# A residual kept in DRAM between stages, its SBUF space given to a pool of work tiles

## The chip, the cores and the metric

The kernel runs on one core of a Trainium2 chip. The metric is the device time of one execution in microseconds. TensorE (PE) does the matrix products, VectorE (DVE), ScalarE (ACT) and GpSimd (POOL) the elementwise work; SyncE (SP) issues nearly all transfers, GpSimd those that add while they write.

## What is computed

Two layers over 512 frames of 1024 features, in float32. Each layer has three stages, and behind each stands a layer norm on the residual x:

```python
for i in range(DEPTH):                     # DEPTH = 2, ALPHA = sqrt(2)
    x = layer_norm(ALPHA * x + 0.5 * swiglu(x, gate1[i], up1[i], down1[i]), ...)      # hidden width 2816
    x = layer_norm(ALPHA * x + hybrid_mixer(x, ...), ...)
    ffn = 0.5 * swiglu(x, gate2[i], up2[i], down2[i])
    ple = sigmoid(x @ ple_w_gate[i]) * (p[i] @ ple_w_proj[i])                          # p[i]: 512 x 256
    x = layer_norm(ALPHA * x + ffn + ple, ...)
```

The mixer projects x to 3340 columns and runs three recurrences on them: a retention of 4 heads (with rotary embedding of its queries and keys), a gated linear recurrence of width 384, and a gated delta rule of 6 heads, each in chunks. Their outputs, 1024 wide together, go through w_out.

## The kernel before

**Products.** Every large operand is split into a high part and the rest, so one product of float32 is three matmuls. A weight tile of 128 x 1024 comes from DRAM into one of four raw buffers (`NRAW`), ACT copies the high part into a slot, and VectorE, sometimes GpSimd, or an adding transfer of GpSimd's queue makes the low part in a second slot. The raw buffer is free for the next load when both are done.

**Slots.** Nearly all SBUF space beside constants is a pool of `NSLOT` = 40 slots of 4 KB per partition (128 x 1024 float32). `slots.get` takes the slot that has been free longest, `slots.put` gives one back; two half tiles share a slot (`halves`). Slots hold split weights, the transposed x and its combinations, the hidden units, and all temporaries of the mixer. The residual is apart from this: `xt`, four tiles of 128 frames x 1024, 4 KB each per partition, which live in SBUF for the whole run (L329).

**Planner.** The program is written out by a planner in Python, which keeps an estimated clock for each engine and decides in which order instructions are emitted. The main thread emits the large products (`mm`, L305). Side threads (`spawn`) emit the dependent chains: norms, the delta rule, the gated recurrence, the retention. They give up control at each `yield` and are resumed when their operands should be there. `prefetch` splits further weights while the work on hand is less than a target and slots are free (`can_step`); `room(n)` keeps a side thread from going on before n slots are free; `wait_until` lets the main thread wait, which advances only side threads. The framework below the planner then orders each engine's queue and sets the semaphores: an instruction that is ready can go ahead of earlier ones that are not.

**Stages.** `swiglu` forms the 22 blocks of hidden units with seven products per block, then runs the down projection over 22 blocks: frames 0 to 255 first, frames 256 to 511 seven blocks later (`LAG`). `mixer` projects block by block (`unit`, 24 matmuls of 512 columns each, in the order q, x, l, r, z, g), spawns the chains, and then multiplies with w_out: eight pairs of weight slots for frames 0 to 255, then again for 256 to 383 and 384 to 511. A rotary unit ("r") starts only when five slots are free (L1657). `embed` does the p part and adds it to `xt` (L1758). `norm` does its first instruction on `xt` (L716), then mean, variance, scale and bias in place, then the transposes by TensorE.

**x.** The input x is loaded into `xt` in four transfers of 512 KB, which the code asks for behind the 24th, 27th, 30th and 33rd weight load (L427 to L429).

Of the kernel before, what the change touches and what calls it, by code (L numbers as in the profile page):

```python
# [20 lines left out]
LN_EPS = 1e-5  # L21
LAG = 7
GROUP = 2
NSLOT = 40
NRAW = 4
TARGET = 14.0
LEVELS = (2, 4, 8, 16, 32, 64)
# [82 lines left out]
def tile_trunk(ctx: ExitStack, tc: tile.TileContext, a, out):  # L110
# [215 lines left out]
    id16 = cpool.tile([128, 128], F16, name="id16")  # L326
    cosT = cpool.tile([128, S], F32, name="cosT")
    sinT = cpool.tile([128, S], F32, name="sinT")
    xt = [cpool.tile([128, D], F32, name=f"x{t}") for t in range(4)]  # L329
    cvr = cpool.tile([128, 128], F32R, name="cvr")  # L330
    nea = cpool.tile([128, L, 6], F32, name="nea")
    m8 = cpool.tile([128, 2, L, 3], F32, name="m8")
# [83 lines left out]
    def load_more():  # L416

        while st["loaded"] < len(loads) and (st["loaded"] < NRAW or readers[st["loaded"] - NRAW] == 0):
            src = loads[st["loaded"]]
            r = raw_tile()  # L420
            dst = r.rearrange("p (g c) -> p g c", g=2) if len(src.shape) == 3 else r[:, 0:src.shape[1]]
            nc.sync.dma_start(out=dst, in_=src)
            raws.pop(st["loaded"] - 1 - NRAW, None)
            if st["loaded"] == 12:
                consts()
                spawn(rotary_tables())
            if st["loaded"] in (24, 27, 30, 33):  # L427
                t = (st["loaded"] - 24) // 3
                nc.sync.dma_start(out=xt[t], in_=a["x"][t * 128:(t + 1) * 128, :])  # L429

    def add_one():

# [267 lines left out]
    def free_xT():  # L700
        for kp in range(4):
            slots.put(xh[kp], xl[kp])
            xh[kp] = xl[kp] = None

    def norm(t, acc, c, gb, out=None, halves_done=None, kind="whole"):


        x = xt[t]
        bs = small.tile([128, 2, 6], F32, tag="bs", name="bs")
        mv = small.tile([128, 2], F32, tag="mv", name="mv")  # L710
        rs = small.tile([128, 1], F32, tag="rs", name="rs")
        for h in range(2):
            while halves_done is not None and halves_done[0] <= h:
                yield
            s = slice(h * 512, (h + 1) * 512)
            stt(x[:, s], acc[h], c / ALPHA, x[:, s], MUL, ADD)  # L716
            ps.put(acc[h])
            if halves_done is not None:
                nc.vector.bn_stats(out=bs[:, h, :], in_=x[:, s])
        yield  # L720
        if halves_done is None:
            for h in range(2):
                nc.vector.bn_stats(out=bs[:, h, :], in_=x[:, h * 512:(h + 1) * 512])
        nc.vector.bn_aggr(out=mv, in_=bs)
        spend("D", 1300, [mv], [x])
        rsqrt(rs, mv[:, 1:2], LN_EPS / ALPHA ** 2)
        yield
        if halves_done is not None:
            for h in range(2):
                s = slice(h * 512, (h + 1) * 512)  # L730
                stt(x[:, s], x[:, s], mv[:, 0:1], gb[0][:, s], SUB, MUL)
                stt(x[:, s], x[:, s], rs, gb[1][:, s], MUL, ADD)
                nc.sync.dma_start(out=out[t * 128:(t + 1) * 128, s], in_=x[:, s])
            slots.put(gb[0], gb[1])
            return
        stt(x, x, mv[:, 0:1], gb[0], SUB, MUL)
        yield
        stt(x, x, rs, gb[1], MUL, ADD)
        gb[2] -= 1
        if gb[2] == 0:  # L740
            slots.put(gb[0], gb[1])
        if out is not None:
            nc.sync.dma_start(out=out[t * 128:(t + 1) * 128, :], in_=x)
            return
        yield
        names = [f"A{1 + t // 2}{q}" for q in (1, 2)]
        keep_raw, parts = kind != "whole", True
        while kind == "whole" and xh[0] is None:
            if len(slots.free) >= 8:
                new_xT()  # L750
            else:
                yield
        while kind != "whole" and names[0] not in quad and names[0] not in xr:
            if len(slots.free) >= 4 * parts + 2 * keep_raw:
                for nm in names:
                    if parts:
                        new_quad(nm)
                    if keep_raw:
                        xr[nm] = slots.get([128, 4, 256], F32)
            else:  # L760
                yield
        c = slice(t * 128, (t + 1) * 128) if kind == "whole" else slice(t % 2 * 128, t % 2 * 128 + 128)
        for q in range(2):
            yield from free_bank()
            p = bank()
            pv = p.rearrange("p (k t) -> p k t", k=4)
            for k in range(4):
                f = (4 * q + k) * 128
                ptr(pv[:, k, :], x[:, f:f + 128], ident)
            for i in range(2):  # L770
                src = pv[:, 2 * i:2 * i + 2, :]
                if kind == "whole":
                    hi, lo = xh[2 * q + i][:, :, c], xl[2 * q + i][:, :, c]
                elif parts:
                    hi, lo = (quad[names[q]][i][:, :, j, c] for j in range(2))
                else:
                    continue
                act(hi, src)
                tt(lo, src, f32(hi), SUB)
            if keep_raw:  # L780
                act(xr[names[q]][:, :, c], pv)
            ps.put(p)
            yield


    def swiglu(l, nm, pend, out=None, kind="whole"):
# [116 lines left out]
        for j in range(MT):  # L903
            ws[j] = take()
            if j:
                if j + 1 < MT:
                    split_h(j + 1)
                down(j, (0, 1))
            else:
                split_h(1)  # L910
                down(0, (0, 1))
                last.run("T4")
                free_quads()
            if j >= LAG:
                if j == LAG:
                    get_acc(acc, (2, 3))
                if j == LAG + 3:
                    gb = load_gb(l, nm)
                if j == MT - 1:
                    ths = [spawn(norm(t, acc[t], 0.5, gb, out, kind=kind), urgent=True) for t in (0, 1)]  # L920
                down(j - LAG, (2, 3))
                drop(j - LAG)
# [52 lines left out]
    def mixer(l, pend):  # L975
# [708 lines left out]
        for k in ks:  # L1684
            need(k, first)
            ws[k] = take()
            wo(k, (0, 1))
        spare[0] = 0
        in_mixer[0] = False
        gb = load_gb(l, "ln_mix")  # L1690
        ths = [spawn(norm(t, acc[t], 1.0, gb, kind="both"), urgent=True) for t in (0, 1)]
        for t in (2, 3):
            get_acc(acc, (t,))
            for k in ks:
                need(k, second)
                wo(k, (t,))
                if t == 3:
                    slots.put(*ws[k])
                    slots.put(oT[k])
            ths.append(spawn(norm(t, acc[t], 1.0, gb, kind="both"), urgent=True))  # L1700
# [4 lines left out]
    def embed(l, pend):  # L1705
# [12 lines left out]
        for half in range(2):  # L1718
# [34 lines left out]
            for t in tiles:  # L1753
# [3 lines left out]
                    ps.put(acc[t][h])  # L1757
                tt(xt[t], xt[t], sg[t], ADD)  # L1758
                slots.put(sg[t])
        slots.put(ph, pl)  # L1760
        wait([mix])

# [190 lines left out]
```

## Time and profile before

| | |
|---|---|
| median of 3 runs | 2166.35 us (2161.36 to 2168.34) |
| the profiled execution | 2159.74 us, of which its span is 2158.0 us |
| PE busy | 2115.7 us, 98% |
| DVE, ACT, POOL busy | 1417.5, 1114.7, 343.3 us |
| moved by transfers | 268.38 MB |

The profile is of one execution; its times count from the start of its span. A busy matmul has a modelled end, so matmuls that wait for one another can still read as busy. The stages can be told by the shape of the matmuls: 256 columns in the gate and up products, 512 in the down projections and most of the mixer. In the first layer the mixer runs from about 350 to 673 us, in the second from about 1425 to 1745 us.

### The profile page before, as it was taken

The numbers are of one execution on the slowest core, as the hardware profiler recorded it, in microseconds if no ns is written. First come the engines' busy times: TensorE is split into PE (matmuls) and PEld (weight loads), VectorE is DVE, ScalarE is ACT, GpSimd is POOL, SyncE is SP. The second block draws the span as 40 slices with busy tenths as digits, with TensorE's granted clock in tenths as the row PEclk, the third lists the DMA queues.
The fourth block names the chain that finished last, engine by engine and source line by source line (L and its number), as shares of the span: only waits on it lengthen the run. The fifth ranks groups of instructions, "written<-read, shape, count | busy, mean of one in ns | idle before, by whom it ended". The sixth has DMA issues, their size and how long they took to land.

```text
span 2158.0 us, 35722 instructions
## 1 busy us (share of the span) xinstructions
PE 2115.7 (98%) x14264; PEld 1905.0 (88%) x14264; DVE 1417.5 (66%) x2415; ACT 1114.7 (52%) x1880; POOL 343.3 (16%) x325
## 2 busy tenths in 40 slices
PE   8999999999999999999999999999999999999998
PEld 7999988977778899998899998889777889999986
DVE  7766636878767766673486665378787677666634
ACT  7666532657334666662266664335564247666530
POOL 3111001233221111100011110012333111111000
PEclk9999999999999999999999999999999999999999
DMA  9776532210133576763247765322102336766621
GB/s 283 178 177 171 162 118 79 79 47 11 59 115 113 127 173 165 176 179 115 83 117 172 174 169 164 106 84 69 38 21 66 98 113 146 187 167 165 182 88 40
DMA packets 104343, 268.38 MB, mean 124 GB/s; under 512 B 9328, under 2 KB 11376, under 8 KB 104176
## 3 DMA queue, kind: packets, MB, share of 16 engines
q1 hardware_dynamic: 80416, 201.07, 28.5%
q0 software_dynamic: 23760, 65.02, 16.8%
q8 instruction: 112, 1.84, 0.3%
q14 instruction: 55, 0.45, 0.1%
HBM read 198.95 MB, written 2.10 MB: 93 GB/s over the span
## 4 chain that ended last, share of the span: by engine, by line
PE 86%; DVE 7%; DMA 3%; ACT 2%; POOL 1%; issue 1%; SPq 0%; DVEq 0%; POOLq 0%; ACTq 0%
PE p L305 78%; PE p L259 6%; DVE s L235 4%; PE p L263 2%; DMA raw<-in_wgu_dram 1%; ACT s L217 1%; DMA s<-in_xT_dram 1%; DMA s<-raw 1%; POOL fs L692 1%; DVE s L239 1%; DMA raw<-in_win_fm_dram 0%; ACT L217 0%; DVE x L239 0%; DVE s L1404 0%; POOL s L235 0%
## 5 line engine op out<-in xcount | busy, mean ns | idle before, releaser
L305 PE MATMUL p<-s,s 128*128 128x256 f32 (+1 forms) x12048 | 1945.1, 320 | 14.0 <-ACT s L217 12.6
L305 PEld LDWEIGHTS p<-s,s 128*128 128x128 f32 x12048 | 1710.5, 191 | 170.6 <-ACT s L217 14.2
L217 ACT ACTIVATE s<-raw 128x1024 fp32r<-128x1024 f32 (+2 forms) x521 | 462.1, 911 | 316.9 <-PE p L305 235.4
L235 DVE TENSOR_TENSOR s<-s,s 128x1024 fp32r<-128x1024 f32 (+4 forms) x433 | 383.9, 908 | 182.7 <-ACT s L217 148.0
L217 ACT ACTIVATE s<-s 128x512 fp32r<-128x512 f32 (+5 forms) x485 | 336.6, 709 | 322.0 <-DVE s L235 164.8
L235 DVE TENSOR_TENSOR s<-raw,s 128x1024 fp32r<-128x1024 f32 (+3 forms) x351 | 334.5, 958 | 245.2 <-ACT s L217 191.6
L217 ACT ACTIVATE s<-p 128x256 f32<-128x256 f32 (+5 forms) x740 | 279.0, 407 | 316.2 <-PE p L305 121.7
L436 POOL DMA_DIRECT2D s<-raw x165 | 143.2, 872 | 881.2 <-ACT s L217 694.2
L235 DVE TENSOR_TENSOR s<-p,s 128x256 f32<-128x256 f32 (+4 forms) x376 | 157.1, 432 | 73.9 <-PE p L305 48.3
L259 PE MATMUL p<-s,s 128*128 128x128 f16 (+6 forms) x1496 | 154.2, 250 | 7.8 <-DVE s L235 6.7
L235 DVE TENSOR_TENSOR s<-raw 128x512 f32<-128x512 f32 x168 | 115.0, 686 | 68.7 <-PE p L305 65.0
L692 POOL TENSOR_TENSOR rs<-rs,half_neg 128x1 f32<-128x1 f32 x24 | 34.8, 1450 | 537.5 <-DVE rs L244 537.5
L259 PEld LDWEIGHTS p<-s,s 128*128 128x128 f32 (+1 forms) x680 | 89.9, 195 | 21.6 <-issue 6.3
L239 DVE SCALAR_TENSOR_TENSOR s<-p,vecs,s 128x255 f32<-128x255 f32 (+5 forms) x128 | 69.3, 550 | 19.7 <-PE p L263 14.8
L217 ACT ACT_TABLE_LOAD x48 | 61.6, 1283 | 14.5 <-DVE tails L250 7.2
L235 DVE TENSOR_TENSOR s<-s,p 128x512 fp32r<-128x512 f32 (+3 forms) x92 | 45.7, 502 | 16.6 <-PE p L259 12.9
L259 PEld LDWEIGHTS <-s 128*128 128x128 f16 x816 | 37.4, 101 | 20.7 <-issue 11.5
L235 DVE TENSOR_TENSOR s<-p,lvm 128x512 f16<-128x512 f32 x72 | 48.2, 683 | 10.6 <-PE p L259 10.2
L235 POOL TENSOR_TENSOR s<-s,cst 128x512 f32<-128x512 f32 x26 | 36.8, 1417 | 96.1 <-DVE s L235 70.0
L239 DVE SCALAR_TENSOR_TENSOR x<-p,x 128x512 f32<-128x512 f32 x48 | 31.5, 682 | 29.2 <-PE p L305 29.0
L263 PE MATMUL p<-cst,s 128*128 128x128 f32 x172 | 33.0, 290 | 9.6 <-ACT s L217 5.3
L263 PEld LDWEIGHTS p<-cst,s 128*128 128x128 f32 x172 | 20.5, 145 | 17.5 <-ACT s L217 6.1
(103 smaller groups left out, 663.3 us busy)
## 6 DMA issues: line engine op xcount, KB each, us to landing
raw<-in_wgu_dram SPq DMA_DIRECT2D x172, 512.0 KB, 4.6
raw<-in_ffn_w_down_dram SPq DMA_DIRECT2D x88, 512.0 KB, 3.6
s<-raw POOLq DMA_DIRECT2D x83, 512.0 KB, 5.4
raw<-in_win_fm_dram SPq DMA_DIRECT2D x48, 512.0 KB, 3.6
s<-raw POOLq DMA_DIRECT2D x82, 256.0 KB, 4.2
raw<-in_w_out_dram SPq DMA_DIRECT2D x16, 512.0 KB, 3.6
raw<-in_ple_w_gate_dram SPq DMA_DIRECT2D x16, 512.0 KB, 4.0
s<-in_xT_dram SPq DMA_DIRECT2D x4, 512.0 KB, 6.3
```

What stands on the lines that cost most here:

```text
L217: nc.scalar.activation(out=out, in_=in_, func=func, **kw)
L235: (eng or nc.vector).tensor_tensor(out=out, in0=in0, in1=in1, op=op)
L239: nc.vector.scalar_tensor_tensor(out=out, in0=in0, scalar=scalar, in1=in1, op0=op0, op1=op1)
L259: nc.tensor.matmul(out=out, lhsT=lhsT, rhs=rhs, start=start, stop=stop)
L263: nc.tensor.transpose(out, in_, idn)
L305: nc.tensor.matmul(out=out, lhsT=lhsT, rhs=rhs, start=start, stop=stop, skip_group_check=resumed)
L436: nc.gpsimd.dma_start(out=out, in_=in_, accum_op=ADD)
L692: nc.gpsimd.tensor_tensor(out=dst, in0=dst, in1=e, op=POW)
```

## The change

`xt` is no longer held in SBUF. Four tiles in DRAM (`xd`) keep the residual. `fetch_x(t)` takes a slot and loads tile t into it (the first time from the input), `keep_x(t)` writes the tile to DRAM and gives the slot back. The pool grows from 40 to 44 slots, which is the 16 KB per partition that `xt` had.

- Feed-forward: the four tiles are fetched at iterations `LAG + 4` to `LAG + 7` of the down projection (11 to 14 of 0 to 21).
- Mixer: tiles 0 and 1 are fetched within the products of w_out as soon as five slots beside the spare four are free, at the latest before the norms are spawned; tiles 2 and 3 each just before their own products.
- Norms: after the transposes of a tile the norm keeps it, save after the mixer, where the embedding uses `xt` next and keeps it itself. The last norm writes the output and keeps nothing.

In all 24 fetches, four of which take the place of the loads of the input, and 20 keeps, of 512 KB each.

```diff
-NSLOT = 40
+NSLOT = 44
...
-    xt = [cpool.tile([128, D], F32, name=f"x{t}") for t in range(4)]
+    dpool = ctx.enter_context(tc.tile_pool(name="kept", bufs=1, space=bass.MemoryType.DRAM))
+    xd = [dpool.tile([128, D], F32, name=f"xd{t}") for t in range(4)]
+    xt = [None] * 4
+    x_in = [True] * 4
...
-            if st["loaded"] in (24, 27, 30, 33):
-                t = (st["loaded"] - 24) // 3
-                nc.sync.dma_start(out=xt[t], in_=a["x"][t * 128:(t + 1) * 128, :])
...
+    def fetch_x(t):
+        xt[t] = slots.get([128, D], F32)
+        nc.sync.dma_start(out=xt[t], in_=a["x"][t * 128:(t + 1) * 128, :] if x_in[t] else xd[t])
+        x_in[t] = False
+
+    def keep_x(t):
+        nc.sync.dma_start(out=xd[t], in_=xt[t])
+        slots.put(xt[t])
+        xt[t] = None
...
@@ norm, after the transposes
+            if q == 1 and kind != "both":
+                keep_x(t)
...
@@ swiglu, down projection
+                if LAG + 4 <= j < LAG + 8:
+                    fetch_x(j - LAG - 4)
...
@@ mixer
             ws[k] = take()
+            for t in (0, 1):
+                if xt[t] is None and len(slots.free) >= 5 + spare[0]:
+                    fetch_x(t)
             wo(k, (0, 1))
         spare[0] = 0
         in_mixer[0] = False
+        for t in (0, 1):
+            if xt[t] is None:
+                wait_until(lambda: slots.free)
+                fetch_x(t)
...
         for t in (2, 3):
             get_acc(acc, (t,))
+            wait_until(lambda: slots.free)
+            fetch_x(t)
...
@@ embed
                 tt(xt[t], xt[t], sg[t], ADD)
                 slots.put(sg[t])
+                keep_x(t)
```

## Rows read from the trace of the kernel before

**Rows 1.** The page's head and its part 1: busy time of the engines.

```profile
span 2158.0 us, 35722 instructions
...
PE 2115.7 (98%) x14264; PEld 1905.0 (88%) x14264; DVE 1417.5 (66%) x2415; ACT 1114.7 (52%) x1880; POOL 343.3 (16%) x325
```

**Rows 2.** The page's part 4: the chain that ended last, shares by engine.

```profile
PE 86%; DVE 7%; DMA 3%; ACT 2%; POOL 1%; issue 1%; SPq 0%; DVEq 0%; POOLq 0%; ACTq 0%
```

**Rows 3.** Windows: stretch, its us, busy us (x instructions) per engine, clock, DMA share, GB/s.

```profile
280.00:300.00 20.00, 20.00 (x90) 16.57 (x89) 7.89 (x9) 6.81 (x9) 0.00 (x0) 1.00 0.30 88
```

**Rows 4.** PE timeline, 0 to 62 us; in brackets idle time before, and its releaser.

```profile
37.51 0.73 PE L305 MATMUL p<-s,s 128*128 128x256 f32 x4 [0.33 <-DMA s<-raw]
39.74 12.50 PE L305 MATMUL p<-s,s 128*128 128x256 f32 x102 [1.50 <-ACT s L217]
53.15 0.98 PE L305 MATMUL p<-s,s 128*128 128x256 f32 x6 [0.91 <-ACT s L217]
54.80 7.45 PE L305 MATMUL p<-s,s 128*128 128x256 f32 x60 [0.68 <-DVE s L235]
```

**Rows 5.** The chain in order of time, first 60 us: start, us, what.

```profile
30.78 12.35 DMA s<-raw
...
43.25 8.42 DMA raw<-in_wgu_dram
```

**Rows 6.** DMA issues of the whole run: KB each, median us from issue to landing.

```profile
raw<-in_wgu_dram SPq DMA_DIRECT2D x172, 512.0 KB, 4.6
...
s<-raw POOLq DMA_DIRECT2D x83, 512.0 KB, 5.4
...
x<-in_x_dram SPq DMA_DIRECT2D x4, 512.0 KB, 12.1
...
out_dram<-x SPq DMA_DIRECT2D x3, 512.0 KB, 2.6
```

**Rows 7.** SP's timeline, 28 to 36 us.

```profile
30.83 2.17 SPq L429 DMA_DIRECT2D x<-in_x_dram  x4
```

**Rows 8.** Windows of line L305 alone: stretch, us, PE, PEld, clock, DMA share, GB/s.

```profile
515.00:532.00 17.00, 0.00 (x0) 0.00 (x0) 0.80 0.00 1
1586.50:1603.50 17.00, 0.00 (x0) 0.00 (x0) 0.80 0.01 1
```

**Rows 9.** Windows of all engines, first mixer: PE, PEld, DVE, ACT, POOL, clock, DMA.

```profile
515.00:532.00 17.00, 14.21 (x124) 12.79 (x123) 13.93 (x32) 15.87 (x31) 7.83 (x8) 0.80 0.00 1
532.00:565.00 33.00, 29.57 (x186) 23.82 (x185) 30.62 (x59) 13.16 (x27) 10.49 (x8) 0.97 0.21 65
565.00:600.00 35.00, 34.70 (x200) 29.46 (x198) 22.01 (x46) 14.29 (x23) 9.42 (x9) 0.98 0.21 60
600.00:648.00 48.00, 45.45 (x244) 37.01 (x245) 31.01 (x77) 12.97 (x25) 7.82 (x7) 0.93 0.36 119
```

**Rows 10.** SP's timeline, 470 to 560 us.

```profile
477.71 0.33 SPq L422 DMA_DIRECT2D raw<-in_win_fm_dram  x1
...
534.78 18.01 SPq L422 DMA_DIRECT2D raw<-in_win_fm_dram  x3
```

**Rows 11.** What SP's queue waited for, 470 to 640 us: total, times, longest.

```profile
SPq L422 <- DVE s L235: 126.5, 13, 56.7
```

**Rows 12.** Windows of instructions on x alone: PE, PEld, DVE, clock, DMA.

```profile
380.00:648.00 268.00, 0.14 (x2) 0.00 (x0) 0.00 (x0) 0.97 0.19 61
```

**Rows 13.** The chain in order of time: start of ffn2, start of the second layer.

```profile
739.57 9.42 DMA raw<-in_wgu_dram
...
1110.85 6.86 DMA raw<-in_wgu_dram
```

**Rows 14.** PE timeline, 1095 to 1130 us, with the idle time before.

```profile
1125.58 4.69 PE L305 MATMUL p<-s,s 128*128 128x256 f32 x37 [1.26 <-ACT s L217]
```

**Rows 15.** Groups of VectorE, 520 to 600 us: xcount | busy, mean ns | idle before.

```profile
L235 DVE TENSOR_TENSOR s<-raw,s 128x1024 fp32r<-128x1024 f32 x7 | 8.7, 1244 | 0.5 <-ACT s L217 0.4
...
L235 DVE TENSOR_TENSOR s<-p,cosT 128x512 f32<-128x512 f32 x3 | 2.0, 677 | 0.0
```

## The prediction

> **What bounds the kernel now.** The page comes first [rows 1]: TensorE is busy for 2115.7 us of a span of 2158.0, so idle time alone leaves 42 us to win, both ends of the run included. A busy TensorE is not one at its peak, so the second view is the chain that ended last [rows 2]: 86% of it runs through PE, 7% through VectorE, 3% through DMA. The stages of the feed-forward blocks are closed: a window of 20 us there holds 90 matmuls of 512 columns at full clock, 222 ns each [rows 3], with nothing between them. More slots can give nothing there, since the operands are in time already. What is left lies in three places, which I looked for in the idle gaps of the PE timeline and in the windows: the first 60 us, the two mixers, and the seams between stages.
>
> *The first 60 us.* The PE timeline shows four gaps after 37 us, of 0.33, 1.50, 0.91 and 0.68 us, together 3.42 us [rows 4]. The chain there runs through two transfers, an accumulate of 12.35 us and a weight load of 8.42 us [rows 5]; over the run these take 5.4 and 4.6 us [rows 6]. What is different just then is that the four loads of x go out at 30.83 us, one behind the other [rows 7], and take 12.1 us each to land [rows 6].
>
> *The mixers.* From 515 to 532 us, and again from 1586.5 to 1603.5 in the second layer, the line that does all large products (L305) has not one matmul [rows 8]. In those 17 us TensorE does 124 small matmuls of the side threads, its granted clock averages 0.80, and ACT (15.87 us) and VectorE (13.93 us) carry the chain [rows 9]. Weights are not far away: the queue issues a load of w_in at 477.71 and the next one at 534.78 [rows 10], and of that it waits 56.7 us in one piece for VectorE to split a raw tile [rows 11]. So raw tiles lie there full and are not split. By the code a split asks two slots of the planner, and a rotary unit (L1657) only starts with five free. I read this as a shortage of slots, and it is the place where the change should act; that ACT and VectorE are at 93% and 82% in the same 17 us speaks against it.
>
> **The change part by part.**
>
> *Slots.* x is not touched by any engine's arithmetic from 380 to 648 us [rows 12] (the two matmuls there are the last of a transpose), and the change puts it in DRAM for just such stretches. So the four tiles are really there for the mixer; from the fetch to the next keep the pool has 40 left, as before. Four slots hold two split weights, which are two units of 24 matmuls of 512 columns: 2 x 24 x 0.222 = 10.7 us of TensorE work [rows 3] that can start where L305 has none. A unit also wants slots for its result, so one unit, 5.3 us, is the lower end of what I expect of the mechanism, 10.7 the upper. I take 8 us per layer, 16 in all. If a mixer only swaps one wait for another it is 0, the bound on that side.
>
> *Clock.* [...] I put none of it in the sum, because the clock is also below full at 600 to 648 us (0.93), where L305 is at work. [...]
>
> *The loads of x at the start go.* The first fetch is now asked for in the down projection of the first block, at iteration 11 of 22. 2 MB leave a stretch where transfers set the chain. The two slow transfers were 12.35 - 5.4 = 7.0 and 8.42 - 4.6 = 3.8 us over their usual time [rows 5, 6], more than the 3.42 us of gaps, so these can all close. I take -3 us; bounds 0 and -3.4.
>
> *Fetches.* 24 of 512 KB, four of which replace the old ones. In the feed-forward blocks they are asked for seven iterations ahead of the norm, 7 x 24 x 0.222 = 37 us. In the mixer tiles 0 and 1 are asked for with the products of w_out, at most 96 x 0.222 = 21 us ahead, tiles 2 and 3 at least 48 x 0.222 = 10.7 us ahead. Landing takes 3 to 5 us for such sizes, 12.1 at the most crowded [rows 6]. All hidden; if a slot came free late, the first instruction of the norm would hold up VectorE, with the splits behind it, by some us per stage. None in the sum.
>
> *Keeps.* 20 writes of 512 KB on SP's queue, each behind the last write of x by VectorE; behind it in the queue are weight loads. A late keep holds the loads back by about the norm's own last instructions, some 1 to 3 us, and the loads themselves wait far longer for raw tiles [rows 11]. The framework also orders a queue's transfers by when it thinks they are ready: the x loads went out at 30.8 us, though the code asks for them behind the 24th weight load. The slot is free when the write has landed, 2.6 us by the nearest row, the output's write [rows 6]. What can cost is the seam: the keeps behind the first layer's last norm and behind the embedding fall where the first loads of the next block are on the chain, 6.86 us at 1110.85 and 9.42 at 739.57 [rows 13]. Two keeps there take 2 x 2.6 = 5 us of the same engines, and a seam has little to hide that in: TensorE stands still for 1.26 us just behind the first of the two [rows 14]. Over both seams that is 0 to some 10 us; I take +2, near the lower end, because a load that is late by 2 us mostly meets operands prepared ahead. [...]
>
> *Sum.* -3 - 16 + 2 = -17 us on the profiled execution's 2159.74. That execution is 6.6 us below the median of 2166.35 and just under the lowest run; I put the same difference on the median: **2149 us**. About 6.5 us, 0.3%, is what a measurement of this kernel can tell from no change; the runs shown spread over 7 us.
>
> **The rivals.**
>
> *A, no change.* The gap in the mixer is a dependent chain on ACT and VectorE, and the large products only move within the mixer: whatever TensorE does earlier, it then waits for the side threads at the end. For it: ACT 93% and VectorE 93% busy in 515-532 and 532-565. Against it: VectorE is idle for 13 of 35 and 17 of 48 us after that [rows 9], so the end is not its bound. -3 + 2: 2165 us. The same time follows if the four slots are swallowed by deeper prefetch.
>
> *B, slower.* VectorE is the bound from 532 to 565 (30.62 of 33 us [rows 9]). Two units moved ahead bring it two splits of weights of 1.24 us, and three further passes of about 0.68 each (the cosine product's row) [rows 15]: 2 x 3.3 = 6.6 us in front of the delta threads, in either layer. If the delta threads, not the retention, are what the last products of w_out wait for, this comes out at the end: +13.2 - 3 + 2 = +12, 2178 us. It decides if the 30 us of VectorE idle after 565 lie beyond that chain.
>
> [...]
>
> *D, contention takes it.* The mixers give 16, but both seams lose 7.0 us, as the accumulate beside the loads of x did [rows 5, 6]: -3 - 16 + 14 = -5, 2161 us, within what can't be told.
>
> **How the numbers follow.** Forecast (2140 to 2158) 0.50; A 0.18; D 0.07; B 0.13; C 0.12. The likeliest gives 2149. The range goes from 2131, below most of C, to 2170, above A and D with the spread of the runs; B and a tail of C stay out, under 2 in 10. The forecast's own range is 2140 to 2158. Faster by over 0.3% is the forecast and C with a little of D: 0.63. The same is A, most of D and an edge of the forecast: 0.22. Slower is B and a tail of A: 0.15.
>
> **What would show it.** L305 should have some 24 to 48 matmuls in the 17 us where it has none, and the clock there should be nearer to full. The 57 us between two weight loads in the mixer should shrink. The gaps at 37 to 55 us should be gone, with the accumulate at its usual 5 us. The mixer should be about 8 us shorter from its first product to the embedding's. Reads of x from DRAM should land over 5 us ahead of the norm's first instruction. I am wrong if the mixer is as long as before with L305 moved, if VectorE shows a wait for x, or if the gap of 1.26 us at the second layer's start grows by more than 2 us.

## The result, and the profile after

| | before | after |
|---|---|---|
| median of 3 runs | 2166.35 us | 2187.02 us (2184.68 to 2190.61) |
| the profiled execution, its span | 2159.74, 2158.0 us | 2187.02, 2185.2 us |
| moved by transfers | 268.38 MB | 289.36 MB |

The ratio is 1.0107 (95% interval 1.0076 to 1.0138): slower by 21 us by the medians, 23 by the ratio, where 17 us of gain were forecast. The page of the kernel after, its head, its busy times, its chain by engine and the new transfers, answers to [rows 1, 2, 6]:

```profile
span 2185.2 us, 35799 instructions
...
PE 2125.2 (97%) x14264; PEld 1914.1 (88%) x14264; DVE 1418.6 (65%) x2413; ACT 1125.1 (51%) x1886; POOL 341.4 (16%) x327
...
PE 77%; DVE 9%; DMA 6%; ACT 4%; POOL 2%; issue 2%; SPq 0%; DVEq 0%; ACTq 0%; POOLq 0%
...
xd<-s SPq DMA_DIRECT2D x20, 512.0 KB, 3.1
s<-xd SPq DMA_DIRECT2D x20, 512.0 KB, 3.4
```

The work of each engine is what it was. What grew in the chain is DMA, from 3% to 6%, VectorE, from 7% to 9%, and ScalarE, from 2% to 4%: TensorE is fed later. To see where, take from each trace the start of the same matmul of L305, the k-th of its width (counted from 0, here and below), and subtract the kernel before. The differences of those differences say what each stretch lost (+) or won (-), in us:

```text
                       start  mixer 1  2nd ffn  its rest  layer 2  mixer 2  2nd ffn  rest    sum
after                  +1.8    -2.7    +10.6     -0.9     +6.6     -0.8    +12.5    +0.2   +27.3
embed_stays     (e1)   +1.9    -7.4     +0.0     -0.5     +6.6     -4.9     +0.8    +0.1    -3.4
late_return     (e2)   +3.6    -2.4     +5.3     -0.7     +8.0     -0.6     +8.3    +0.3   +21.8
pool_queue      (e3)   +2.1    -2.3    +10.4     -0.9     +6.9     -1.5    +11.9    -0.1   +26.5
writes_alone    (e4)   +1.3    +0.2     +1.3     +0.1     +0.0     +1.7     +1.7    +0.2    +6.5
mixer_only      (e5)   +3.7    -2.1     -0.1     +0.0     +0.1     -1.5     +0.0    +0.0    +0.1
x_late          (e6)   +0.0    +3.6     -0.1     +0.4     +0.1     +4.5     +0.2    +0.0    +8.7
four_idle       (e7)   +2.3    +4.7     -0.1     -0.3     +0.0     +2.3     +0.0    +0.0    +8.9
return_at_fetch (e8)   +2.3    -1.9     +1.3     -0.8     +5.8     -1.7     +2.2    +0.4    +7.6
forty_outside   (e9)   +6.3    -2.8     +1.4     -0.3     +0.0     -3.2     +1.3    +0.0    +2.7
forty_at_start  (e10)  -0.2    -2.7     -0.1     -0.2     +0.0     -1.3     +0.0    +0.3    -4.2
38_slots        (e11)  -2.8   +20.9     -0.1     -2.8     +0.0    +24.7     +0.6    -0.1   +40.4
```

The stretches end at the matmuls of 256 columns with the numbers 1800, 2800, 4400, 4800 and 6800 and of 512 columns with the numbers 1344 (the first embedding's end), 3264 (the second's) and 3839. Each row is one profiled execution. The row of after is the result in one line: both mixers together win 3.5 us, and three stage starts lose 29.7. All three follow a norm whose four slots went back to the pool: the two second feed-forward blocks (behind the embedding) and the second layer.

What two executions of one program differ by is shown by e6, whose trace has the work of before in the order of before (see there): 0.2 us or less at the stage starts, but 3.6 and 4.5 us in the mixers. So for the mixers one row is too little, and the profile of before lies 6.6 us under its median. The eight rows with four more slots in the mixer (after, e1, e2, e3, e5, e8, e9, e10) average -3.0 and -1.9, the four without (before at 0, e4, e6, e7) +2.1 and +2.1: by that the mixers win 5.2 and 4.1 us, about 9 in all.

**The mixers.** The same windows as [rows 8, 9], first of L305 alone, then of all engines:

```profile
515.00:532.00 17.00, 7.33 (x22) 3.91 (x22) 1.00 0.09 32
...
600.00:648.00 48.00, 19.25 (x69) 13.07 (x69) 0.83 0.32 101
```

```profile
515.00:532.00 17.00, 16.13 (x144) 13.14 (x144) 13.48 (x31) 8.77 (x23) 6.28 (x6) 1.00 0.09 32
...
600.00:648.00 48.00, 47.47 (x247) 40.08 (x247) 32.05 (x85) 10.06 (x23) 6.78 (x6) 0.83 0.32 101
```

Where L305 had nothing it now has 22 matmuls, at a clock of 1.00 instead of 0.80. But 600 to 648 has lost products (69 for 82), and its clock fell from 0.93 to 0.83. The 768th matmul of 512 columns starts 20.0 us earlier (512.4 for 532.4), the 960th still 18.0 earlier, the 1056th, in the products of w_out, only 0.8. Products were moved, and towards the mixer's end most of the time was given back. SP's timeline there and its longest wait for VectorE (total, times, longest), for [rows 10, 11]:

```profile
469.96 80.14 SPq L425 DMA_DIRECT2D raw<-in_win_fm_dram  x4
```

```profile
SPq L425 <- DVE s L235: 922.1, 251, 31.6
```

Of these four loads the last two stand furthest apart, at 517.8 and 549.8. Raw tiles are split sooner: the longest wait is 31.6 us, not 56.7. The shortage of slots was real.

**The stage starts.** The PE timeline, in brackets the idle time before and its releaser:

```profile
41.02 29.19 PE L305 MATMUL p<-s,s 128*128 128x256 f32 x220 [3.77 <-ACT s L217]
...
747.22 4.58 PE L305 MATMUL p<-s,s 128*128 128x256 f32 x36 [2.12 <-DVE s L235]
753.53 16.28 PE L305 MATMUL p<-s,s 128*128 128x256 f32 x132 [1.73 <-ACT s L217]
770.89 5.30 PE L305 MATMUL p<-s,s 128*128 128x256 f32 x42 [1.07 <-DVE s L235]
...
788.74 11.48 PE L305 MATMUL p<-s,s 128*128 128x256 f32 x81 [2.42 <-ACT s L217]
...
1133.96 9.26 PE L305 MATMUL p<-s,s 128*128 128x256 f32 x72 [0.84 <-ACT s L217]
1147.14 13.91 PE L305 MATMUL p<-s,s 128*128 128x256 f32 x96 [3.92 <-ACT s L217]
```

The four gaps at 37 to 55 us [rows 4] are one of 3.77. Behind the embedding there are now several, 7.34 us in the four shown. At the second layer's start the gap of 1.26 [rows 14] is now 0.84, and 72 matmuls behind it stands a new one of 3.92. The kernel before had none there:

```profile
1125.58 44.61 PE L305 MATMUL p<-s,s 128*128 128x256 f32 x363 [1.26 <-ACT s L217]
```

Here a stop costs more than its idle time. In the 10 us in which the stops of 3.77 and 3.92 us end the clock averages 0.70 and 0.76, and 0.90 in the next 10 us behind the second, where before has 1.00. Windows of all engines, first after, then before:

```profile
40.00:50.00 10.00, 8.98 (x56) 8.98 (x57) 7.47 (x14) 7.90 (x14) 1.79 (x2) 0.70 0.52 118
1140.00:1150.00 10.00, 6.08 (x40) 5.88 (x40) 3.03 (x5) 4.30 (x9) 0.86 (x1) 0.76 0.73 208
1150.00:1160.00 10.00, 10.00 (x78) 10.00 (x77) 5.79 (x9) 6.00 (x11) 1.72 (x2) 0.90 0.77 162
```

```profile
40.00:50.00 10.00, 10.00 (x85) 10.00 (x85) 8.46 (x14) 7.01 (x12) 0.91 (x1) 1.00 1.05 317
1140.00:1150.00 10.00, 10.00 (x84) 9.92 (x84) 6.35 (x11) 4.43 (x9) 0.86 (x1) 1.00 0.74 184
```

The 96 matmuls behind the stop of 3.92 us take 145 ns each, the 363 of before 123. Over the three starts TensorE stands idle for 7.9, 4.3 and 8.1 us more than before, 20.3 of the 29.7; of the other 9.4 these 96 matmuls are 2.1.

The chain in order of time, for [rows 13], shows what stands in front of the gaps at 747:

```profile
737.52 7.67 DMA xd<-s
...
745.21 1.04 DVE s L235 x2
746.27 0.64 ACT s L217 x2
746.91 5.22 DMA raw<-in_wgu_dram
...
753.53 6.16 PE p L305 x50
```

A write of x is on the chain for 7.67 us: VectorE's next split goes into the slot that the write still reads. In the second layer the same piece is at 1823.43 and takes 7.82. The view of waits says it for the whole run, in total, times and longest:

```profile
DVE s L235 <- DMA xd<-s: 8.1, 2, 4.3
...
ACT s L217 <- DMA xd<-s: 3.3, 3, 1.5
```

There is no wait for a read of x by any engine.

### The profile page after: what moved, and what is told of

Read it like the earlier page. It is cut to its first block, busy times and chain, and to the rows that moved or that the text cites. A ratio compares the mean times of both kernels' runs of the same rounds, so it can differ in the third digit from the quotient of the medians.

```text
span 2185.2 us, 35799 instructions
## 1 busy us (share of the span) xinstructions
PE 2125.2 (97%) x14264; PEld 1914.1 (88%) x14264; DVE 1418.6 (65%) x2413; ACT 1125.1 (51%) x1886; POOL 341.4 (16%) x327
## 2 busy tenths in 40 slices
DMA packets 110104, 289.36 MB, mean 132 GB/s; under 512 B 9968, under 2 KB 12016, under 8 KB 109936
## 4 chain that ended last, share of the span: by engine, by line
PE 77%; DVE 9%; DMA 6%; ACT 4%; POOL 2%; issue 2%; SPq 0%; DVEq 0%; ACTq 0%; POOLq 0%
PE p L305 69%; PE p L259 7%; DVE s L235 6%; DMA raw<-in_wgu_dram 3%; ACT s L217 3%; DVE s L239 2%; PE p L263 2%; POOL s L235 1%; DMA xd<-s 1%; DMA raw<-in_win_fm_dram 1%; ACT L217 1%; DMA s<-in_xT_dram 1%; DVE fs L235 0%; POOL fs L692 0%; POOL rk L692 0%
## 5 line engine op out<-in xcount | busy, mean ns | idle before, releaser
L305 PE MATMUL p<-s,s 128*128 128x256 f32 (+1 forms) x12048 | 1954.7, 321 | 34.7 <-ACT s L217 25.5
L305 PEld LDWEIGHTS p<-s,s 128*128 128x128 f32 x12048 | 1717.7, 192 | 192.8 <-ACT s L217 28.8
L235 DVE TENSOR_TENSOR s<-s,s 128x512 fp32r<-128x512 f32 (+4 forms) x441 | 399.4, 928 | 216.1 <-ACT s L217 193.3
L217 ACT ACTIVATE s<-s 128x1024 fp32r<-128x1024 f32 (+5 forms) x485 | 335.4, 710 | 321.0 <-PE p L305 155.7
L235 DVE TENSOR_TENSOR s<-raw,s 128x512 f32<-128x512 f32 (+2 forms) x349 | 330.9, 953 | 227.0 <-ACT s L217 134.7
L235 DVE TENSOR_TENSOR s<-p,s 128x256 f32<-128x256 f32 (+3 forms) x376 | 156.7, 433 | 76.6 <-PE p L305 45.5
L259 PE MATMUL p<-s,s 128*128 128x64 f16 (+6 forms) x1448 | 151.1, 256 | 0.0
L259 PEld LDWEIGHTS p<-s,s 128*128 128x128 f32 (+1 forms) x632 | 88.3, 215 | 14.1 <-issue 7.0
L263 PE MATMUL p<-cst,s 128*128 128x128 f32 x332 | 56.0, 282 | 11.3 <-POOL s L235 4.4
L263 PEld LDWEIGHTS p<-cst,s 128*128 128x128 f32 x332 | 40.5, 144 | 24.4 <-POOL s L235 5.4
L235 DVE TENSOR_TENSOR s<-s,p 128x128 f32<-128x128 f32 (+2 forms) x92 | 46.3, 504 | 23.5 <-PE p L259 21.3
L239 DVE SCALAR_TENSOR_TENSOR s<-p,s 128x512 f32<-128x512 f32 x48 | 31.5, 682 | 28.9 <-PE p L305 28.8
L259 PEld LDWEIGHTS <-s 128*128 128x128 f16 x816 | 34.7, 98 | 15.5 <-issue 10.2
```

The source lines that it names most:

```text
L217: nc.scalar.activation(out=out, in_=in_, func=func, **kw)
L235: (eng or nc.vector).tensor_tensor(out=out, in0=in0, in1=in1, op=op)
L239: nc.vector.scalar_tensor_tensor(out=out, in0=in0, scalar=scalar, in1=in1, op0=op0, op1=op1)
L259: nc.tensor.matmul(out=out, lhsT=lhsT, rhs=rhs, start=start, stop=stop)
L263: nc.tensor.transpose(out, in_, idn)
L305: nc.tensor.matmul(out=out, lhsT=lhsT, rhs=rhs, start=start, stop=stop, skip_group_check=resumed)
```

## The experiments

The ratios are to runs of the kernel before on the same chip.

**e1, the embedding keeps x in SBUF.** After, without the keeps behind the embedding and the fetches of the second feed-forward blocks.

```diff
-                if LAG + 4 <= j < LAG + 8:
+                if LAG + 4 <= j < LAG + 8 and nm == "ln_ffn1":
@@ embed
-                keep_x(t)
```

> The changed kernel, but x stays in its slots from the mixer's fetch to the second feed-forward's norm: no keep in the embedding, no fetch in that down projection; 8 writes and 8 reads fewer, and 40 free slots instead of 44 in the second feed-forward. If the embedding's keeps are what costs at the start of the second feed-forward (by their place in SP's queue, their landing or the bandwidth they take), the 10.4 and 12.6 us lost there go: about 2187 - 23 = 2164 us, and no stop of PE over 1 us between 735 and 800 us. If the loss comes from the larger pool or another order of instructions in general, most of it stays: 2180 us or more.

Median 2164.83 us, ratio 1.0001 (0.9985 to 1.0018). The two starts behind the embedding lose 0.0 and 0.8 instead of 10.6 and 12.5: most of the loss hangs on these 8 keeps and the slots that they free. The second layer's start still loses 6.6.

**e2, the slots come back late.** After, but the embedding's four slots return to the pool at block 4 of the next gate and up products.

```diff
+    def write_x(t):
+        nc.sync.dma_start(out=xd[t], in_=xt[t])
+        held.append(xt[t])
+        xt[t] = None
...
+            if m == 4 and held:
+                slots.put(*held)
+                held.clear()
@@ embed
-                keep_x(t)
+                write_x(t)
```

> The changed kernel, but the slots that the embedding's keeps free go back to the pool only at the fifth block of hidden units, some 40 us later; the writes themselves stay where they are in SP's queue. Theory landing: VectorE waits in order for the write to DRAM because it is the next to fill the slot (4.3 us at 741 us, behind a write that took 7.7 us); then most of the 23 us at the two starts go, about 2167 us, and nothing waits for xd there. Theory queue: the writes hold up the weight loads on SP behind VectorE's additions; then the loss stays, 2183 to 2188 us. Theory bandwidth: stays as well.

Median 2181.5, ratio 1.0074 (1.0045 to 1.0104). No engine waits for a write of x there any more, and of 10.6 and 12.5 us the starts still lose 5.3 and 8.3. So the reuse of a slot whose write hasn't landed is worth up to 5.3 and 4.2 us (the four slots are also missing for four blocks), and half or more stays. It comes late: a gap of 2.25 us after the slots are back, on the PE timeline of e2.

```profile
752.85 20.54 PE L305 MATMUL p<-s,s 128*128 128x256 f32 x168 [2.18 <-ACT s L217]
773.56 10.62 PE L305 MATMUL p<-s,s 128*128 128x256 f32 x84 [0.18 <-ACT s L217]
786.44 7.46 PE L305 MATMUL p<-s,s 128*128 128x256 f32 x60 [2.25 <-ACT s L217]
```

**e3, the keeps on GpSimd's queue.** After, with one line changed.

```diff
-        nc.sync.dma_start(out=xd[t], in_=xt[t])
+        nc.gpsimd.dma_start(out=xd[t], in_=xt[t])
```

> The changed kernel with all keeps issued from GpSimd's queue instead of SP's; slots, order and traffic as the planner had them. Theory queue: weight loads on SP are no longer behind a write that waits for VectorE, most of the 23 us go: about 2165 us. Theory landing: SP is free, but the freed slots are still filled only when the write has landed: 2180 us or more, and if GpSimd's accumulating transfers now wait behind the writes, up to 10 us more than 2187.

Median 2186.77, ratio 1.0105 (1.0081 to 1.0128); the starts lose 10.4, 6.9 and 11.9. The place in SP's queue, where a keep stands before weight loads, isn't the cause; e4 and e8 leave the writes there and lose at most 2.2 us per start.

**e4, the writes alone.** Before, with the 20 writes of x added and nothing else: x stays in SBUF, 40 slots.

```diff
...
+            if q == 1 and kind != "both":
+                nc.sync.dma_start(out=xd[t], in_=x)
...
@@ embed
+                nc.sync.dma_start(out=xd[t], in_=xt[t])
```

> The kernel before, x in SBUF and 40 slots, with only the 20 writes of x to DRAM added at the places of the keeps; nobody reads them and no slot is freed by them. Theory landing: 2166 us, as before. Theory queue or bandwidth: slower by the loss at the seams, 2180 to 2195 us. Between the two: how much of it the write itself costs.

Median 2172.34, ratio 1.003 (1.0007 to 1.0053). The starts lose 1.3, 0.0 and 1.7. The bytes are not free, but they are a small part of what the starts lose. (This profile is 6.1 us under the median of its runs, so the writes may cost something more that its row doesn't show.)

**e5, DRAM only ahead of the mixer.** After, but only the norm behind the first feed-forward block keeps; behind the embedding and the layer's last norm x stays.

```diff
-            if q == 1 and kind != "both":
+            if q == 1 and kind == "whole":
...
-                if LAG + 4 <= j < LAG + 8:
+                if LAG + 4 <= j < LAG + 8 and xt[j - LAG - 4] is None:
@@ embed
-                keep_x(t)
```

> The changed kernel with x in DRAM for the mixers alone: kept behind each first feed-forward's norm, fetched in the products of w_out, and then in its slots until the next layer's first norm. 8 writes and 12 reads, four of them of the input. With x held in the embedding there was no loss at the second feed-forward but still 6.6 us at the second layer's start. If the keeps behind the first layer's last norm cause those, they go: 2165 - 6.6 = 2158 us, 0.3% below the kernel before. If they come from the order that the larger pool gives, they stay: 2165 us.

Median 2164.02, ratio 0.9993 (0.998 to 1.0006). All three starts are as before (-0.1, 0.1, 0.0), the second layer's too. The mixers win 2.1 and 1.5. The loss at the second layer's start is gone, but the median is 2164, not 2158: against e1 the starts lose 7.4 us less, and the ratio falls by only 0.0008, 1.7 us. Where the rest went stays open.

**e6, x loaded late.** Before, with the four loads of x asked for in the first down projection, as after has them.

```diff
-            if st["loaded"] in (24, 27, 30, 33):
-                t = (st["loaded"] - 24) // 3
-                nc.sync.dma_start(out=xt[t], in_=a["x"][t * 128:(t + 1) * 128, :])
...
+                if l == 0 and nm == "ln_ffn1" and LAG + 4 <= j < LAG + 8:
+                    t = j - LAG - 4
+                    nc.sync.dma_start(out=xt[t], in_=a["x"][t * 128:(t + 1) * 128, :])
```

> The kernel before, x in SBUF and 40 slots, with nothing changed but the four loads of the input x, which are asked for at iterations 11 to 14 of the first down projection. My forecast gave 3 us for this: PE's gaps between 37 and 55 us, 3.4 us in all, close, 2163 us. Rival: ACT's own queue sets those gaps (one gap of 3.8 us behind ACT stood there in the changed kernel): 2166 us, and a gap of 3 to 5 us between 37 and 42 us.

Median 2162.22, ratio 0.999 (0.9972 to 1.0007); the start is 0.0 us off. But the loads did not move. The framework sent them where they went in the kernel before [rows 7], as SP's timeline shows:

```profile
30.65 2.72 SPq L918 DMA_DIRECT2D x<-in_x_dram  x4
```

Every engine has the instructions of before, in the order of before. So e6 says nothing about the loads of x; it is a second profile of the kernel before. Two gaps took the place of four in it:

```profile
37.51 0.74 PE L305 MATMUL p<-s,s 128*128 128x256 f32 x4 [1.42 <-DMA s<-raw]
40.20 22.02 PE L305 MATMUL p<-s,s 128*128 128x256 f32 x168 [1.96 <-ACT s L217]
```

1.42 and 1.96 are 3.38 us, where there were 3.42 [rows 4]: the gaps of one program differ between these two executions, their sum hardly. The mixers are 3.6 and 4.5 us longer than in the first profile, with nothing changed.

**e7, the mixer's four slots left idle.** e5, with four slots taken out of the pool for the length of the projections.

```diff
@@ mixer, at its start
+        idle = [slots.get([128, D], F32) for _ in range(4)]
+        for s_ in idle:
+            nc.vector.memset(s_[:, 0:1], 0.0)
@@ mixer, ahead of the first fetch
+            if idle:
+                slots.put(*idle)
+                idle = []
```

> The mixer-only kernel with four slots held back, unused, from the second half of the mixer's first products to the start of w_out, so that the mixer has 40 slots as before; four small memsets are added. If the four slots are what moves the large products forward, the 768th matmul of 512 columns, which came 20 us earlier with them, is back near its old place, and the mixer has its old length: 3 to 8 us per layer slower than mixer-only. If the order alone does it, nothing moves.

Median 2167.01, ratio 1.0006 (0.9991 to 1.002). The window of L305 that after had filled is empty again, at the clock of before [rows 8]:

```profile
515.00:532.00 17.00, 0.00 (x0) 0.00 (x0) 0.79 0.00 1
```

The 768th matmul of 512 columns is at 537.6 us, 23.0 later than in e5 (514.6). It is the four slots that move the products. The mixers are 6.8 (4.7 + 2.1) and 3.8 (2.3 + 1.5) us longer than in e5. By the medians e7 is 3.0 us slower than e5, by the profiled executions 8.9, so these two figures are too high; the direction is the same.

**e8, the slots come back at the fetch.** After, with e2's `write_x` in the embedding, but the four slots return just before the next fetch, in the down projection. All transfers stay; one read of x in each of the two stages goes out early, right behind the writes, at 743.7 and 1820.0 us.

```diff
+                if j == LAG + 4 and held:
+                    slots.put(*held)
+                    held.clear()
                 if LAG + 4 <= j < LAG + 8:
                     fetch_x(j - LAG - 4)
@@ embed
-                keep_x(t)
+                write_x(t)
```

> The changed kernel with the slots that the embedding's keeps free withheld until the fetch in the next down projection: the second feed-forward then never uses them, the writes stay. Theory landing and reuse: only the writes themselves are left, 1.5 us per start as they cost in the kernel before, so 2187 - 23 + 3 = 2167 us. If the place of the writes in SP's queue or their bandwidth were the rest of what a later return left (5.3 and 8.3 us): 2178 us or more.

Median 2168.11, ratio 1.002 (1.0004 to 1.0036). The starts behind the embedding lose 1.3 and 2.2 us, as much as the writes alone; e2 less e8 is 4.0 and 6.1. The second layer's start, whose four slots still go back at once, loses 5.8.

**e9, 40 slots everywhere outside the mixers.** e8, and the same for the layer's last norm; four slots are also held from the start to the first fetch.

```diff
+    held = [slots.get([128, D], F32) for _ in range(4)]
+    for s_ in held:
+        nc.vector.memset(s_[:, 0:1], 0.0)
...
-            if q == 1 and kind != "both":
+            if q == 1 and kind == "whole":
                 keep_x(t)
+            elif q == 1 and kind == "blocks":
+                write_x(t)
```

> The change with all its writes and fetches, but with 40 slots outside the mixers: four slots are held from the start to iteration 11 of the first down projection, and the slots of x behind the embedding and behind the first layer's last norm go back to the pool only there. Theory: the four more free slots at a stage's start are what is left of the loss, through the order in which splits stand in ScalarE's and VectorE's queues. It expects the start to lose at most 1 us instead of 1.9, the two second feed-forward starts 1 to 2 us as with the return at the fetch, the second layer's start about 0 instead of 5.8, and a median of 2160 to 2165. Rival: the DRAM traffic itself costs there. It expects the second layer's start to lose 5 us or more again, and a median of 2168.

Median 2162.65, ratio 0.9986 (0.9967 to 1.0004): 1.2% less than after by the ratios, with every one of its transfers. The three stage starts lose 1.4, 0.0 and 1.3; the start of the run, which was to lose 1 us at most, loses 6.3 (see e10). The second layer's start is the clean one, since no engine waits for a write of x there in after either. PE timelines, first e8, then e9:

```profile
1126.11 9.25 PE L305 MATMUL p<-s,s 128*128 128x256 f32 x72 [0.84 <-ACT s L217]
1139.18 20.99 PE L305 MATMUL p<-s,s 128*128 128x256 f32 x156 [3.81 <-ACT s L217]
```

```profile
1125.73 3.22 PE L305 MATMUL p<-s,s 128*128 128x256 f32 x24 [1.02 <-ACT s L217]
1130.21 30.04 PE L305 MATMUL p<-s,s 128*128 128x256 f32 x245 [1.25 <-ACT s L217]
```

The gap of 3.8 us is there with 44 slots and not with 40, all else alike. What makes it is read from ScalarE's timeline, first after, then e9:

```profile
1135.68 2.01 ACT L217 ACTIVATE s<-raw 128x1024 fp32r<-128x1024 f32 x2
...
1145.76 1.06 ACT L217 ACTIVATE s<-raw 128x1024 fp32r<-128x1024 f32 x1 [5.70 <-DMA raw<-in_wgu_dram]
1146.72 0.36 ACT L217 ACTIVATE s<-p 128x256 f32<-128x256 f32 x1
```

```profile
1142.75 2.01 ACT L217 ACTIVATE s<-raw 128x1024 fp32r<-128x1024 f32 x2 [0.28 <-PE p L305]
```

With slots to spare ScalarE splits weights ahead until it reaches one whose load is still under way. It stands for 5.70 us, and behind it in its queue stands the short copy of an accumulator, 0.36 us at 1146.72, which ends at 1147.08; TensorE resumes at 1147.14, behind ScalarE. In e9 the pair of splits comes at 1142.75, later, and waits for TensorE alone. In after ScalarE's queue kept its order: TensorE had stopped at 1143.22, so the product to copy was done by then, and the copy came 3.50 us later, behind the split.

**e10, 40 slots at the start too.** e5, with four slots held from the start of the run to the first fetch (the `held` of e9).

```diff
+    held = [slots.get([128, D], F32) for _ in range(4)]
+    for s_ in held:
+        nc.vector.memset(s_[:, 0:1], 0.0)
...
+                if j == LAG + 4 and held:
+                    slots.put(*held)
+                    held.clear()
```

> The kernel that keeps x in DRAM only ahead of the mixer, with four slots held from the start of the run to iteration 11 of the first down projection. No transfer is added or taken away by this. Theory: free slots decide the start too, so the 3.7 us that the first 840 matmuls of 256 columns lost go (0 to 1 us lost, or up to 3 gained as the forecast had it), the mixers gain 3 to 4 us as before, and the median is 2159 to 2162. Rival: the start loses because the loads of x are gone from the queue there, which moved the loads behind them; it expects 3 to 4 us lost at the start again and a median of 2164.

Median 2155.88, ratio 0.9966 (0.995 to 0.9982): faster than both kernels, and faster than expected. In its profile the start is 0.2 us earlier than in the kernel before, and the mixers win 2.7 and 1.3. But the start can't be credited to the held slots. Up to the embedding's products e9 and e10 have the same matmuls, in the same order, and the same order of transfers on SP's queue (one load of x at 35.92 and 30.94 us, three from about 280 us on); still one lost 6.3 us at the start and the other won 0.2. Their PE timelines, first e9, then e10:

```profile
46.03 16.21 PE L305 MATMUL p<-s,s 128*128 128x256 f32 x116 [7.08 <-ACT s L217]
```

```profile
40.01 22.24 PE L305 MATMUL p<-s,s 128*128 128x256 f32 x170 [3.23 <-ACT s L217]
```

So a start can differ by more than the forecast's term for it with the same order of work. Whether that comes with the execution or with the program, one profile of each can't say. The medians of e9 and e10 differ by 6.8 us over 12 runs each, and past the start the profiles differ by only 0.4 (2.7 - 6.3 and -4.2 + 0.2), which would fit a difference that stays with the program. It is left open.

**e11, 38 slots.** Before, with one constant changed.

```diff
-NSLOT = 40
+NSLOT = 38
```

> The kernel before with 38 slots instead of 40 and nothing else. Theory (more free slots put later splits ahead in the queues at a stage's start): the starts of the second feed-forward blocks and of the second layer are no later after their norm than before, 0 or up to 3 us sooner, while the mixers lose 2 to 6 us each. Rival (a start has the slots that it needs and fewer only hurt): the starts lose as well, by 2 us or more each.

Median 2202.58, ratio 1.018 (1.0156 to 1.0204). The starts lose -0.1, 0.0 and 0.6: two slots fewer cost nothing there. The mixers lose 20.9 and 24.7, far over the 2 to 6 expected.

## Why the prediction was wrong

**The step that failed is the keeps, +2**, with the sentence before it that more slots can give nothing in the feed-forward blocks. Nothing to win was read as nothing to lose. The text counted two seams, but the embedding stands in both layers, so there are three. They lost 29.7 us, in three parts:

- the writes themselves, 1.3 + 2.2 = 3.5 us (e8; e4 and e9 give 3.0 and 2.7). This is about the +2 of the sum.
- slots used again before their write has landed, at most 5.3 + 4.2 = 9.5 us (after less e2; the waits for these writes in after, 8.1 and 3.3 us, are of that size). The text saw that a slot is free only when the write has landed, but took 2.6 us from the output's write [rows 6]; on the chain the landing took 7.67 and 7.82, and VectorE's queue stood behind it.
- four more free slots at a stage's start, 4.0 + 6.1 + 6.6 = 16.7 us (e2 less e8; the second layer's start of after, which is 0.1 in e5 and 0.0 in e9). This is the largest part, and no step of the prediction had it. At the second layer's start the four writes landed in 2.6 us each, as the prediction had it, no engine waited for one, and 6.6 us were lost all the same. That free slots are the cause is shown by e8 and e9, which change only when slots return (and, with the slots, when one read goes out). That it works through the order of ScalarE's queue is read from the timelines of the second layer's start; no run changed the order by itself.

The times bear these rows out. From after to e1, e2, e8, e9 and e10 the losses at the three starts fall by 22.3, 8.1, 20.4, 27.0 and 29.8 us, the ratios by 23.0, 7.1, 18.8, 26.2 and 30.5 (as us of 2166.35). Only e5 falls short, 24.7 for 29.7.

**The mixers, -16**, was mis-sized; they gave 3.5 in the row of after, and about 9 by the rows with and without the slots, just under the step's lower end of 5.3 a layer. The mechanism was right up to the place where it acts: 22 matmuls in the empty window, a clock of 1.00 in it, a shorter wait for splits, and e7 undoes all of it. But matmuls 20 us sooner in the middle are not 8 us at the end. For the greater part of their 20 us, as rival A had it, the large products only moved within the mixer. The bounds too were of the wrong kind, since a slot isn't worth so many matmuls: two fewer cost 20.9 and 24.7 us, four more won about 5 and 4.

The clock's low stretch is at another place than before (0.80 at 515 to 532 there, 0.83 at 600 to 648 in after). After and e1 have the same matmuls in the same order up to the embedding's products, yet the 1056th of 512 columns is at 652.7 us in one and 648.0 in the other. The line of the small matmuls (L259), from 590 to 650 us, first after, then e1:

```profile
590.00:650.00 60.00, 32.33 (x180) 28.82 (x180) 0.83 0.32 104
```

```profile
590.00:650.00 60.00, 28.08 (x180) 24.85 (x180) 0.91 0.33 102
```

The same 180 matmuls take 32.33 us at a mean clock of 0.83 and 28.08 at 0.91; the difference of 4.25 us is near the 4.7. With the large products gone early, the clock averages less at that end of the mixer: over these 60 us seven of the eight profiles with the four slots have 0.83 (e1 has the 0.91), the four without them 0.92 to 0.94. So the clock at the mixer's end differs by the execution, and is lower with the slots than without. The step on the clock put nothing in the sum because the clock was below full at 600 to 648 as well (0.93), and that caution was right: at 515 to 532, now with 22 large matmuls, the clock is 1.00 for 0.80, and at 600 to 648, where TensorE is busy for 47.47 of 48 us, it is 0.83 for 0.93.

**The start, -3**, gave +1.8 in the profile, and no run tested the term by itself, since the loads of x stayed in e6. In the seven kernels that start as after does (after, e1, e2, e3, e5, e7, e8), the loads go out from 275 us on, and the start is 1.8 to 3.7 us later instead of 3 sooner. One link of the step holds: without the loads beside it, the accumulate that goes out at 30.2 us in after lands in 7.7 us, where the one at 30.78 took 12.35. The gaps did not close with it. One of 3.77 us behind ScalarE took the place of 3.42 in four, and from 40 to 50 us, where it ends, the clock is 0.70 where it was 1.00. Whether that is for the four more slots or for the loads that follow sooner stays open.

**The fetches, 0**, were right: no engine waits for a read of x.

**The rivals.** It ended on B's side, slower, but not by B's mechanism: VectorE displaced in the mixer would have made the mixers longer. D named the right place, the seams, with 7.0 us each, from the accumulate that took 12.35 us beside the loads of x instead of 5.4. Of its two, the one behind the embedding lost 10.6, of which the transfers alone are 1.3, and the second layer's start 6.6, of which they are nothing (e4, e9). The embedding of the second layer, which it didn't count, lost 12.5, of which the transfers are 2.2. C, faster than the forecast, has no run on its side: none shows that a mixer gets shorter by the clock. What the profiles show is a clock of 1.00 for 0.80 at 515 to 532, of 0.83 for 0.93 at 600 to 648, and both mixers together 3.5 us shorter in the row of after.

**What was to show it.** L305 in the empty window (22 matmuls, just under the 24 to 48), the clock there, and the shorter wait came true. The gaps at 37 to 55 did not go, and the mixer was not 8 us shorter. Of the three signs of an error the first came, a mixer nearly as long with L305 moved. VectorE did wait for x, but for its writes. The gap of 1.26 did not grow; the sign looked at the right stage, but the loss stood in a new gap 72 matmuls further on.

## What to carry to other kernels

A slot whose write to DRAM has just been issued is not free space (the writes of x took 2.6 to 7.8 us to land): hold it until it is needed, as e8 does. The pool here already hands out the slot that has been free longest, and that was not enough. A pool is also a limit on how far ahead each engine's queue may run, and space given to all stages loosens that limit where it was doing good; give it to the stage that lacks it and take it back behind it, as e9 and e10 do. And products that move 20 us forward in the middle of a stage say nothing about its end until one has seen what its last products wait for. A stop of TensorE can cost more than its length: behind the one of 3.92 us 96 matmuls took 145 ns each instead of 123. And an edit of the program is a test only if the trace shows that it moved what it was to move: in e6 it didn't.

## What was not expected of the hardware

Executions with the same order of matmuls differ at the start by 6.5 us (e9, e10) and in the first mixer's end by 4.7 us (after, e1), the second with the granted clock at 0.83 and 0.91 in the same 60 us. Two executions of one program (before, e6) differ by 3.6 and 4.5 us in the mixers. A stop of TensorE of 3.92 us ended at 1147.14; the clock was 0.76 from 1140 to 1150 us and 0.90 from 1150 to 1160, where the kernel before, without the stop, has 1.00 in both. A write of 512 KB that lands in 3.1 us in the median was on the chain for 7.67 and 7.82 us, each time beside two accumulates of GpSimd's queue, which took 8.3 and 10.1, and 7.4 and 9.5 us to land.
